# A two-layer diffusion block on one core: the rest of the MoE routing is called for inside the first expert block

## The chip, the cores and the metric

The kernel runs on one core of a Trainium2 chip. The metric is the device time of one execution in microseconds (us); the time of the kernel before is the median of three executions.

## The reference, cut to what matters

Two layers (one with a Mamba-2 mixer over 512 tokens, context and latent, one with a retention mixer over the 256 latent tokens), each of them closed by a hierarchical mixture of experts (MoE) in fp32. The routing of the MoE chooses for every token one group of four, then two of its eight experts:

```
g_sel = jnp.argmax(g_logits, -1)
g_gate = take(jax.nn.softmax(g_logits, -1), g_sel)
e_logits = take(e_logits.reshape(n_tok, 4, 8), g_sel)
top_p, top_i = lax.top_k(jax.nn.softmax(e_logits, -1), 2)
top_w = top_p / jnp.sum(top_p, -1, keepdims=True) * g_gate[:, None]
...
out = (silu(x @ gate[e]) * (x @ up[e])) @ down[e]     # each chosen expert e
ffn = sum over the two choices of top_w * out
```

All 32 experts' weights (6 MB each) are read from HBM in each layer.

## The kernel before, in words

A layer's MoE is an object of class `MoE`: `route()` (line 1535) decides where every token goes, `pairs()` (line 1841) runs over the experts, `finish()` and `norms()` close the layer. Layer 0 has four tiles of 128 tokens (`nt` = 4), layer 1 two.

**Routing.** `route()` starts from the logits `lg` of all tokens. VectorE marks the group and the two experts of each token (lines 1575 to 1597; `goh`, `oh1`, `oh2`, their maxima `gm`, `m1`, `m2`). TensorE counts, by products with a triangle and with ones, the number of each token in its expert's queue (tile `pp`), from which VectorE writes `pos`, the slot of each token at each expert (line 1607). `gather_oh` (line 1688) writes the one-hot matrices `oh` of the first four experts, which always stand at places 0 to 3 (line 1609). `places()` (line 1631) sorts the other experts by load: `to` is the permutation from experts to places, `ppe` the product that gives each place its expert. Then `to_places(pos, True)` (lines 1611 and 1656) brings `pos` into the order of places: four transposes (`pat`), a copy by ScalarE (`aT`), a product with `to` for each tile (`pap`), and one more product whose result is kept as `posT` (`pab`). After it come the softmax weights (lines 1613 to 1624: nine VectorE operations and two exponentials) and `to_places(wt, False)` for the weights (line 1625), and `wr`, the weights split into two parts (line 1627).

**Experts.** `pairs()` goes through blocks of two wide experts (64 slots each) or four narrow ones (32 slots each); `p` is the block's number, two blocks share one set of one-hot matrices `G[g]`. The tokens of a block are gathered by products with the one-hots (`gather`, line 1703, tile `px`, copied to `xT` by ScalarE for the one block and VectorE for the other). For block 0 this is done piecewise ahead of the contraction steps of its own products (line 1886: one eighth ahead of steps k = 0 and 1, two eighths ahead of 2, 4 and 6). `gate_up` (line 1753) has eight steps k, each with the gate and up products (`pg`, `pu`) of the block's experts; then follow `hidden_T`, `down` (`pd`) and, a block later, `add` (`pc`, line 1829). `one_hots(1)` is called for ahead of block 0's `gate_up` (line 1885); its tile has one buffer, which `G[0]` holds until `weights(0)` (`pw`, line 1728) has read it. `blocks()` and `base()` (lines 1919 and 1818) come behind block 0's products; `base` runs on GpSimd.

**Order of the work.** Instructions are put in order by a planner when the kernel is built: each engine takes, in the planner's own reckoning of time, the first instruction in program order that is ready. Operations called through `S.T`, `S.V` and `S.A` (class `InOrder`, line 187; they all show line 194 in the profile) are pinned behind the one that stands ahead of them on their engine; all others may move ahead. All of `route()` is pinned so. PSUM tiles of the tag "mm" (`pp`, `pk`, `ppe`, `pat`, `pap`, `pab`, `px`, `pw`, `pb`, `ph`) share two buffers.

**Weights.** `Ring` (line 124) holds 1 MB slots in several pools; SyncE's queue issues one load (line 173) as soon as the products that read the slot's old content are done. The order of the loads is fixed when the kernel is built, and a load that waits holds up those behind it. Behind block 5 stands a branch on a run-time count (line 2008) that lets overfull experts take more blocks; it is not taken here.

Of the kernel before, what the change touches and what calls it, by code (L numbers as in the profile page):

```python
# [12 lines left out]
F32R = mybir.dt.float32r  # L13
# [3 lines left out]
AF = mybir.ActivationFunctionType  # L17
OP = mybir.AluOpType
AX = mybir.AxisListType
# [3 lines left out]
P = 128  # L23
# [173 lines left out]
def col(S, name, a=0, b=None):  # L197
    o, w = CL[name]
    return S.c[:, o + a:o + (w if b is None else b)]
# [1236 lines left out]
FIRST = ((0, 0), (1,))  # L1436
ROWS_AT = (0,)
ROWS_K = (2, 4)


class Expert:
# [30 lines left out]
class MoE:  # L1472
# [62 lines left out]
    def route(self):  # L1535
# [16 lines left out]
        def red(out, in_, op):  # L1552
            V.tensor_reduce(out, in_, AX.X, op)

        def bc(a, k):
            return a[:, :, None].to_broadcast([P, nt, k])
# [51 lines left out]
        V.tensor_scalar(pos, pos, -1024.0, None, op0=OP.add)  # L1608
        self.G = {0: self.gather_oh([(pos[:, :, 0:FIXED], CAP)], col(S, "i64"), V)}
        self.places(pp[:, nt, :], sb16)  # L1610
        self.pos, self.posT = self.to_places(pos, True)

        d, gsum, p2, rd = new(4), new(), new(4), new(4)
        V.tensor_tensor(d, lg4, bc(gm, 4), OP.subtract)
        AC.activation(d, d, AF.Exp)
        red(gsum, d, OP.add)
        V.tensor_tensor(p2, m2, m1, OP.subtract)
        AC.activation(p2, p2, AF.Exp)
        V.scalar_tensor_tensor(rd, p2, 1.0, bc(gsum, 4), op0=OP.add, op1=OP.mult)
        V.reciprocal(rd, rd)  # L1620
        V.scalar_tensor_tensor(rd, rd, 0.5, goh, op0=OP.mult, op1=OP.mult)
        V.tensor_tensor(oh2, oh2, of_group(p2), OP.mult)
        V.tensor_tensor(oh2, oh2, oh1, OP.add)
        V.tensor_tensor(by_group(wt), oh2, of_group(rd), OP.mult)
        self.wt, _ = self.to_places(wt, False)

        self.wr = sb.tile([P, nt, 2, 32], F32R, name="wr")
        V.tensor_copy(self.wr[:, :, 0], self.wt)
        V.tensor_tensor(self.wr[:, :, 1], self.wt, self.wr[:, :, 0].bitcast(F32), OP.subtract)

    def places(self, cn, sb16):

# [20 lines left out]
        self.expert, self.cn = by[:, 0], by[:, 1]  # L1653
        self.reg = {}

    def to_places(self, a, back):

        S, nt, V, T_ = self.S, self.nt, self.S.V, self.S.T
        pt = self.ps([32, nt, 128], "pat", "mm")
        for i in range(nt):  # L1660
            T_.transpose(pt[:, i], a[:, i], col(S, "ident"))
        aT = self.wk2.tile([32, nt * 128], F32, name="aT", tag="os", bufs=2)
        S.A.activation(aT, pt.rearrange("e t c -> e (t c)"), AF.Copy)
        pa = self.ps([P, nt, 32], "pap", "mm")
        for i in range(nt):
            T_.matmul(pa[:, i], aT[:, i * 128:(i + 1) * 128], self.to[:, :32], start=True, stop=True)
        V.tensor_copy(a, pa)
        if not back:
            return a, None
        pb = self.ps([64, self.T], "pab", "mm")  # L1670
        T_.matmul(pb, self.to, aT, start=True, stop=True)
        t = self.sb.tile([64, self.T], BF, name="posT")
        V.tensor_copy(t, pb)
        V.tensor_tensor(t[32:64], pb[32:64], t[32:64], OP.subtract)
        return a, t
# [165 lines left out]
    def pairs(self):  # L1841
# [20 lines left out]
        def part(g, q, nb=2):  # L1862
            self.gather(G[g], [xT[2 * g], xT[2 * g + 1]], q, nb)
# [5 lines left out]
                weights(g)  # L1869
        start(0)  # L1870
        prev = None

        def after(th, W, os_, w, end=False):
            nonlocal prev
# [6 lines left out]
        for p, places in enumerate(order):  # L1881
            g = p // 2 + 1
            W = [Expert(S, self.layer, e, e == WIDE) for e in places]
            if p % 2 == 0 and g < groups:
                G[g] = one_hots(g)
            th = self.gate_up(W, xT[p], None if p else lambda k: part(0, k, 1) if k < 2 else part(0, k // 2) if k % 2 == 0 else None)
            if p == 0:
                self.spread_rows()
            os_ = self.scatter_oh([S.id2[:, e:e + 1] for e in places], s64 if width(p) == CAP else s32)
            if g < groups:  # L1890
                if p == 0:
                    weights(0)
                    self.blocks()
                    self.base()
                if p % 2 == 0:
                    start(g)
                if p > LATE:
                    ahead(p, g)
            after(th, W, os_, ws[p], p == last)
            if g < groups and p <= LATE:  # L1900
                ahead(p, g)
            if p == EXTRA:
                W = [Expert(S, self.layer, WIDE)]
                pw = self.wk.tile([P, self.nt, 1], F32, name="pw")
                nc.vector.tensor_scalar(pw, self.pos[:, :, WIDE:WIDE + 1], float(-CAP), None, op0=OP.add)
                sw = self.wk.tile([P, 1], F32, name="sw")
                nc.vector.tensor_scalar(sw, s64, float(CAP), None, op0=OP.add)
                x, wx = self.block_tokens(self.gather_oh([(pw, CAP)], i64), self.wt[:, :, WIDE:WIDE + 1])
                c = S.id2[:, WIDE:WIDE + 1]
                osx = self.scatter_oh([c, c], sw)  # L1910
                after(self.gate_up(W, x), W, osx, wx)
            if p == REST:
                self.add(*prev)
                prev = None
                self.rest()
# [288 lines left out]
```

## Time and profile before

| | us |
|---|---|
| median of 3 executions (lowest, highest) | 2083.04 (2081.06, 2083.69) |
| the profiled execution | 2084.03 |
| its span, first to last instruction | 2082.2 |
| TensorE busy | 1827.3 (88%) |
| VectorE, ScalarE, GpSimd busy | 1023.1, 508.4, 516.2 |
| mean granted TensorE clock | 0.944 of full |
| read from HBM | 537.51 MB, 261 GB/s over the span |

The profile is of one execution. Busy shares are means over stages with different limits, so the stage of the change is read by itself: the timeline gives start and length of each group of instructions with the idle time before it and what ended that, the windows give busy time, granted clock and DMA rate of a stretch.

### The profile page before, as it was taken

How to read it: one execution, taken by the hardware profiler on the slowest of the kernel's cores; microseconds unless marked ns; L12 is line 12 of the kernel's file. 1: busy time of each engine (PE TensorE's matmuls, PEld its weight loads, DVE VectorE, ACT ScalarE, POOL GpSimd, SP SyncE). 2: the span in 40 equal slices, each digit the busy share in tenths (PEclk: the TensorE clock that was granted, in tenths of full speed). 3: DMA queues.
4: the chain of work that ended last, by engine and by line, in shares of the span. 5: the costliest groups of instructions: out<-in, count | busy, mean ns of one | idle time of the engine just before them, and what ended most of it. 6: DMA issues, size and time to landing. Idle time of an engine off the chain costs nothing. (4 is left out here: it accounts for less than half of the span.)

```text
span 2082.2 us, 24508 instructions
## 1 busy us (share of the span) xinstructions
PE 1827.3 (88%) x9373; PEld 1057.7 (51%) x9373; DVE 1023.1 (49%) x1790; ACT 508.4 (24%) x885; POOL 516.2 (25%) x332
## 2 busy tenths in 40 slices
PE   7798889889985999989999979898896999878886
PEld 4576667567674433334333368786873433312221
DVE  3868687777586243443333475574444332311112
ACT  2655454544212100000000142332232101100000
POOL 1454645444345000000000053464551100000000
PEclk9899999999995999999999989999997999989998
DMA  7332322234843997799999754464364999999996
GB/s 296 105 122 82 132 102 102 100 133 144 284 162 126 382 402 302 300 393 377 409 409 409 302 176 145 164 238 157 125 238 171 377 412 413 413 367 411 414 413 252
DMA packets 137947, 544.42 MB, mean 261 GB/s; under 512 B 10368, under 2 KB 10880, under 8 KB 125152
## 3 DMA queue, kind: packets, MB, share of 16 engines
q1 hardware_dynamic: 137392, 542.57, 67.5%
q8 instruction: 76, 1.25, 0.2%
q14 instruction: 47, 0.39, 0.0%
q10 hardware_dynamic: 432, 0.21, 0.0%
HBM read 537.51 MB, written 5.24 MB: 261 GB/s over the span
## 5 line engine op out<-in xcount | busy, mean ns | idle before, releaser
L428 POOL TENSOR_TENSOR wl<-ringA,wh 128x1024 fp32r<-128x1024 f32 x117 | 293.5, 2523 | 808.3 <-ACT wh L427 800.2
L427 ACT ACTIVATE wh<-ringA 128x1024 fp32r<-128x1024 f32 x120 | 126.1, 1058 | 189.2 <-issue 46.9
L1765 PE MATMUL pg<-ringB,xT 128*32 128x512 f32 (+1 forms) x348 | 123.2, 600 | 4.1 <-DMA ringB<-in_moe_w_gate_up_dram 3.8
L1774 DVE SCALAR_TENSOR_TENSOR th<-th,pg 128x512 f32<-128x512 f32 (+1 forms) x24 | 16.5, 686 | 224.4 <-ACT th L1770 207.8
L1765 PE MATMUL pu<-ringB,xT 128*32 128x512 f32 (+1 forms) x316 | 119.1, 605 | 4.3 <-SPq L2008 2.8
L1770 ACT ACTIVATE th<-pg 128x512 f32<-128x512 f32 (+1 forms) x24 | 14.3, 596 | 433.5 <-PE pg L1765 422.6
L1837 DVE TENSOR_TENSOR tl<-pc,ringB 128x512 f32<-128x512 f32 x136 | 88.9, 685 | 55.0 <-PE pc L1812 53.4
L1805 DVE SCALAR_TENSOR_TENSOR yh<-pd,ws,yh 128x512 fp32r<-128x512 f32 x40 | 30.0, 751 | 173.5 <-ACT yh L1804 171.6
L2064 POOL TENSOR_TENSOR oacc<-oacc,ringE 128x512 f32<-128x512 f32 x1 | 1.6, 1622 | 451.9 <-ACT oacc L194 451.9
L1794 PE MATMUL pd<-ringE,hT 128*32 128x512 f32 (+1 forms) x360 | 103.7, 618 | 6.0 <-ACT hT L1784 3.4
L1794 PE MATMUL pd<-ringB,hT 128*32 128x512 f32 (+1 forms) x304 | 104.0, 630 | 4.1 <-ACT hT L1784 2.4
L1712 PEld LDWEIGHTS px<-oh,hhl 128*128 128x128 f32 x640 | 81.2, 194 | 37.4 <-issue 36.1
L1171 PE MATMUL pin<-u,wh 128*128 128x256 f32 (+1 forms) x256 | 84.3, 330 | 16.6 <-DVE gT L1223 12.3
L724 DVE SCALAR_TENSOR_TENSOR cacc<-pad,cw,cacc 128x512 f32<-128x512 f32 x96 | 94.1, 983 | 6.8 <-ACT cacc L722 6.1
L1765 PE MATMUL pg<-ringE,xT 128*32 128x512 f32 (+1 forms) x240 | 90.3, 613 | 7.5 <-DMA ringE<-in_moe_w_gate_up_dram 6.2
L1812 PE MATMUL pc<-yh,os 128*128 128x512 f32 (+1 forms) x272 | 89.5, 432 | 6.2 <-DVE tl L1837 5.5
L1765 PE MATMUL pg<-ringA,xT 128*32 128x512 f32 (+1 forms) x220 | 93.1, 615 | 1.9 <-DMA ringA<-in_moe_w_gate_up_dram 1.9
L1765 PE MATMUL pu<-ringE,xT 128*32 128x512 f32 (+1 forms) x240 | 91.6, 606 | 3.0 <-DMA ringE<-in_moe_w_gate_up_dram 3.0
L1765 PE MATMUL pu<-ringA,xT 128*32 128x512 f32 (+1 forms) x204 | 91.1, 610 | 3.0 <-DMA ringA<-in_moe_w_gate_up_dram 3.0
L1712 PE MATMUL px<-oh,hhl 128*128 128x256 f32 (+1 forms) x640 | 91.2, 293 | 0.5 <-DVE wsx L1997 0.5
L1838 DVE TENSOR_TENSOR oacc<-oacc,tl 128x512 f32<-128x512 f32 x136 | 88.5, 684 | 0.7
L1765 PE MATMUL pg<-ringF,xT 128*32 128x512 f32 (+1 forms) x204 | 85.0, 607 | 3.6 <-DMA ringF<-in_moe_w_gate_up_dram 3.3
(407 smaller groups left out, 4432.7 us busy)
## 6 DMA issues: line engine op xcount, KB each, us to landing
ringB<-in_moe_w_gate_up_dram SPq DMA_DIRECT2D x79, 1024.0 KB, 17.1
ringE<-in_moe_w_gate_up_dram SPq DMA_DIRECT2D x60, 1024.0 KB, 17.7
ringA<-in_moe_w_gate_up_dram SPq DMA_DIRECT2D x51, 1024.0 KB, 17.6
ringF<-in_moe_w_gate_up_dram SPq DMA_DIRECT2D x47, 1024.0 KB, 17.8
ringE<-in_moe_w_down_dram SPq DMA_DIRECT2D x43, 1024.0 KB, 17.9
ringA<-in_mod_w_dram SPq DMA_DIRECT2D x40, 1024.0 KB, 4.9
ringB<-in_moe_w_down_dram SPq DMA_DIRECT2D x36, 1024.0 KB, 15.7
ringA<-in_ret_in_w_dram SPq DMA_DIRECT2D x24, 1024.0 KB, 5.0
```

The costliest lines, as they stand in the source:

```text
L427: S.split = nc.scalar.activation(hi, w, AF.Copy).ins
L428: (eng or nc.gpsimd).tensor_tensor(lo, w, hi.bitcast(F32), OP.subtract)
L724: nc.vector.scalar_tensor_tensor(acc, pad[:, :, t:t + 256], cw[:, m, t:t + 1], acc, op0=OP.mult, op1=OP.add)
L1171: self.S.nc.tensor.matmul(p, a, self.uh(k)[:, T], start=k == 0, stop=False)
L1712: nc.tensor.matmul(px[:, b, :], self.S.hhl[i][:, m, j * 128:(j + 1) * 128], oh[:, i], start=i == 0 and m == 0, stop=i == nt - 1 and m == 1)
L1765: nc.tensor.matmul(po[o:o + n, :], xT[:, k, a * n:(a + 1) * n], w.get(k)[:, u * 512:(u + 1) * 512], start=k == 0, stop=k == 7)
L1774: nc.vector.scalar_tensor_tensor(th[:m], th[:m], 1.0, pg[:m], op0=OP.add, op1=OP.mult)
L1794: nc.tensor.matmul(pd[u % n][o:o + m, :], hT[:, j, a * m:(a + 1) * m], w.get(8 + j)[:, u * 512:(u + 1) * 512], start=j == 0, stop=j == 3)
L1805: self.S.nc.vector.scalar_tensor_tensor(yl[:, u], p, ws, yh[:, u].bitcast(F32), op0=OP.mult, op1=OP.subtract)
L1812: self.S.nc.tensor.matmul(pc, os_[s, i * 128:(i + 1) * 128], ys[q][s, u % n], start=q == 0, stop=q == 1)
L1837: V.tensor_tensor(t, pc, self.gate(i)[:, c], OP.mult)
L1838: V.tensor_tensor(self.acc(i)[:, c], self.acc(i)[:, c], t, OP.add)
```

## The change

The two moves to place order and the softmax weights leave `route()` and become a generator, `rest_of_route()`. It is advanced ahead of steps k = 1, 2, 4 and 5 of block 0's gate and up products, behind that step's gather. `to_places` is cut in two (`by_expert` does the transposes and the copy). The operations moved are called through `nc.vector`, `nc.scalar` and `nc.tensor`: they are no longer pinned. `one_hots(1)` is called for behind block 0's products. The number of instructions stays the same.

```diff
+ROUTE_K = (1, 2, 4, 5)
@@ route()
-        self.pos, self.posT = self.to_places(pos, True)
+        self.chosen = lg4, gm, m1, m2, goh, oh1, oh2, new, pos, wt
+
+    def rest_of_route(self):
...
+        V, AC = S.nc.vector, S.nc.scalar
...
+        aT = self.by_expert(pos)
 
         d, gsum, p2, rd = new(4), new(), new(4), new(4)
...
         V.tensor_tensor(by_group(wt), oh2, of_group(rd), OP.mult)
-        self.wt, _ = self.to_places(wt, False)
-
-        self.wr = sb.tile([P, nt, 2, 32], F32R, name="wr")
+        yield
+        self.pos, self.posT = self.to_places(pos, aT, True)
+        yield
+        aT = self.by_expert(wt)
+        yield
+        self.wt, _ = self.to_places(wt, aT, False)
+
+        self.wr = self.sb.tile([P, nt, 2, 32], F32R, name="wr")
         V.tensor_copy(self.wr[:, :, 0], self.wt)
         V.tensor_tensor(self.wr[:, :, 1], self.wt, self.wr[:, :, 0].bitcast(F32), OP.subtract)
+        yield
@@ to_places()
+    def by_expert(self, a):
+
+        S, nt = self.S, self.nt
         pt = self.ps([32, nt, 128], "pat", "mm")
         for i in range(nt):
-            T_.transpose(pt[:, i], a[:, i], col(S, "ident"))
+            S.nc.tensor.transpose(pt[:, i], a[:, i], col(S, "ident"))
         aT = self.wk2.tile([32, nt * 128], F32, name="aT", tag="os", bufs=2)
-        S.A.activation(aT, pt.rearrange("e t c -> e (t c)"), AF.Copy)
+        S.nc.scalar.activation(aT, pt.rearrange("e t c -> e (t c)"), AF.Copy)
+        return aT
+
+    def to_places(self, a, aT, back):
+
+        nt, V, T_ = self.nt, self.S.nc.vector, self.S.nc.tensor
@@ pairs()
+        later = self.rest_of_route()
+
+        def first(k):
+            if k < 2 or k % 2 == 0:
+                part(0, k if k < 2 else k // 2, 1 if k < 2 else 2)
+            if k in ROUTE_K:
+                next(later)
...
-            if p % 2 == 0 and g < groups:
+            if p % 2 == 0 and 0 < p and g < groups:
                 G[g] = one_hots(g)
-            th = self.gate_up(W, xT[p], None if p else lambda k: part(0, k, 1) if k < 2 else part(0, k // 2) if k % 2 == 0 else None)
+            th = self.gate_up(W, xT[p], None if p else first)
             if p == 0:
+                G[1] = one_hots(1)
                 self.spread_rows()
```

## Rows read from the trace of the kernel before

**Rows 1.** Windows: length, PE, PEld, DVE, ACT, POOL busy, PE clock, DMA share, GB/s.

```profile
648.40:668.70 20.30, 11.49 (x42) 8.25 (x42) 11.57 (x50) 3.68 (x6) 6.29 (x3) 0.50 0.54 204
668.70:691.70 23.00, 22.86 (x120) 10.91 (x119) 3.40 (x8) 2.02 (x5) 12.35 (x6) 0.96 0.69 256
...
1579.40:1593.50 14.10, 7.25 (x27) 5.10 (x26) 7.58 (x45) 1.44 (x5) 0.00 (x0) 0.50 0.54 219
```

**Rows 2.** Timeline of layer 0: start, length, engine, line, operation, count, idle before.

```profile
648.83 1.43 DVE L194 TENSOR_TENSOR oh<-c,pos 128x256 fp32r<-128x256 f32 x4
651.49 0.60 PE L194 MATMUL ppe<-pl,c 32*128 32x32 f32 x2 [3.16 <-DVE pl L194]
662.34 1.01 PE L194 MATMUL pat<-c,wt 128*32 128x128 f32 x4 [4.37 <-DVE wt L194]
665.87 2.93 PE L1712 MATMUL px<-oh,hhl 128*128 128x256 f32 x12
668.72 1.12 PE L1765 MATMUL pg<-ringX,xT 128*64 128x512 f32 x1
674.41 2.17 PE L1712 MATMUL px<-oh,hhl 128*128 128x256 f32 x16
692.78 1.71 DVE L1697 TENSOR_TENSOR oh<-c,pos 128x128 fp32r<-128x128 f32 x8 [0.52 <-PE pw L1728]
```

**Rows 3.** Timeline of layer 1.

```profile
1579.80 0.76 DVE L194 TENSOR_TENSOR oh<-c,pos 128x256 fp32r<-128x256 f32 x2
1591.50 2.08 PE L1712 MATMUL px<-oh,hhl 128*128 128x256 f32 x8
1593.51 1.98 PE L1765 MATMUL pg<-ringF,xT 128*64 128x512 f32 x4
1615.33 1.08 PE L1765 MATMUL pg<-ringE,xT 128*64 128x512 f32 x4 [0.47 <-ACT xT L1718]
```

**Rows 4.** PE groups by shape, 647 to 669 us, then 1578 to 1592 us: busy, mean, idle.

```profile
L194 PE MATMUL pap<-pl,aT 32*128 32x32 f32 x16 | 3.8, 399 | 1.4 <-ACT aT L194 1.4
L194 PE MATMUL pab<-aT,pl 32*64 32x512 f32 x2 | 2.0, 1083 | 0.0
...
L194 PE MATMUL pap<-pl,aT 32*128 32x32 f32 x8 | 2.1, 402 | 0.9 <-ACT aT L194 0.9
L194 PE MATMUL pab<-aT,pl 32*64 32x256 f32 x2 | 1.1, 656 | 0.0
L194 PE MATMUL pat<-c,wt 128*32 128x128 f32 x2 | 0.6, 396 | 3.5 <-DVE wt L194 3.5
```

**Rows 5.** SyncE's queue: the first weight load that each MoE's products set free.

```profile
674.50 0.37 SPq L173 DMA_DIRECT2D ringX<-in_moe_w_gate_up_dram  x1
...
1598.11 7.35 SPq L173 DMA_DIRECT2D ringF<-in_moe_w_gate_up_dram  x3
```

**Rows 6.** Windows of the expert blocks of both layers, columns as in rows 1.

```profile
690.00:820.00 130.00, 124.59 (x641) 54.27 (x637) 53.04 (x118) 11.97 (x22) 0.00 (x0) 0.98 0.98 389
820.00:840.00 20.00, 20.00 (x99) 10.68 (x99) 2.94 (x4) 1.98 (x3) 0.00 (x0) 0.93 0.32 106
840.00:860.00 20.00, 20.00 (x80) 6.05 (x76) 9.51 (x16) 1.57 (x3) 0.00 (x0) 0.97 0.60 233
...
1640.00:1850.00 210.00, 187.22 (x965) 70.71 (x962) 62.86 (x126) 19.42 (x35) 0.00 (x0) 0.98 1.03 413
```

**Rows 7.** PE's waits from 690 to 820 us, the longest: total, times, longest.

```profile
PE ph L1782 <- DVE th L1775: 2.9, 2, 1.6
```

**Rows 8.** Timeline of GpSimd and VectorE, layer 1, then GpSimd's `base` of layer 0.

```profile
1572.58 0.30 DVE L194 TENSOR_TENSOR xT<-xT 128x64 f32<-128x64 f32 x2
1573.12 4.69 POOL L194 TENSOR_TENSOR hhl<-tok,hhl 128x1024 fp32r<-128x1024 f32 x2 [1.17 <-ACT hhl L194]
1573.36 2.19 DVE L194 TENSOR_TENSOR xT<-xT 128x64 f32<-128x64 f32 x1
...
662.41 4.66 POOL L1825 TENSOR_TENSOR oacc<-oacc,ringB 128x1024 f32<-128x1024 f32 x2 [18.35 <-ACT ringB L1822]
```

More of the change, by code (lines that the diff above doesn't have):

```diff
@@ L1610, in route @@
         self.places(pp[:, nt, :], sb16)
-        self.pos, self.posT = self.to_places(pos, True)
+        self.chosen = lg4, gm, m1, m2, goh, oh1, oh2, new, pos, wt
+    def rest_of_route(self):
+        S, nt = self.S, self.nt
+        V, AC = S.nc.vector, S.nc.scalar
+        lg4, gm, m1, m2, goh, oh1, oh2, new, pos, wt = self.chosen
+        by_group = lambda a: a.rearrange("p t (g e) -> p t g e", g=4)
+        of_group = lambda a: a[..., None].to_broadcast([P, nt, 4, 8])
+        aT = self.by_expert(pos)
         d, gsum, p2, rd = new(4), new(), new(4), new(4)
-        V.tensor_tensor(d, lg4, bc(gm, 4), OP.subtract)
+        V.tensor_tensor(d, lg4, gm[:, :, None].to_broadcast([P, nt, 4]), OP.subtract)
         AC.activation(d, d, AF.Exp)
-        red(gsum, d, OP.add)
+        V.tensor_reduce(gsum, d, AX.X, OP.add)
         V.tensor_tensor(p2, m2, m1, OP.subtract)
         AC.activation(p2, p2, AF.Exp)
-        V.scalar_tensor_tensor(rd, p2, 1.0, bc(gsum, 4), op0=OP.add, op1=OP.mult)
+        V.scalar_tensor_tensor(rd, p2, 1.0, gsum[:, :, None].to_broadcast([P, nt, 4]), op0=OP.add, op1=OP.mult)
         V.reciprocal(rd, rd)
@@ L1654, in places @@
         self.reg = {}
-    def to_places(self, a, back):
-        S, nt, V, T_ = self.S, self.nt, self.S.V, self.S.T
+    def by_expert(self, a):
+        S, nt = self.S, self.nt
         pt = self.ps([32, nt, 128], "pat", "mm")
         for i in range(nt):
-            T_.transpose(pt[:, i], a[:, i], col(S, "ident"))
+            S.nc.tensor.transpose(pt[:, i], a[:, i], col(S, "ident"))
         aT = self.wk2.tile([32, nt * 128], F32, name="aT", tag="os", bufs=2)
-        S.A.activation(aT, pt.rearrange("e t c -> e (t c)"), AF.Copy)
+        S.nc.scalar.activation(aT, pt.rearrange("e t c -> e (t c)"), AF.Copy)
+        return aT
+    def to_places(self, a, aT, back):
+        nt, V, T_ = self.nt, self.S.nc.vector, self.S.nc.tensor
         pa = self.ps([P, nt, 32], "pap", "mm")
```

## The prediction

> **What bounds the kernel now.** I read the windows around the start of each MoE first, then the timeline inside them, then the groups of TensorE there, SyncE's queue, and the windows of the blocks behind. The 20.3 us between the counting products and block 0's first gate product in layer 0 show TensorE busy for 11.49 us at a clock of 0.50 (its lower level, 1.2 GHz); the 23 us behind them show it busy for 22.86 us at 0.96 (nearly all at 2.4 GHz). Layer 1 has the same gap: 14.1 us, 7.25 busy, clock 0.50 [rows 1]. The gap is a chain on one strand: the timeline of layer 0 has TensorE waiting 3.16 us for VectorE's sorting (`ppe`), then 4.37 us for the softmax weights (`pat`), and only then the gathers, which have had their one-hots since 650.26 us (648.83 + 1.43) but start at 665.87; the first product is at 668.72 [rows 2]. In layer 1 the one-hots are there at 1580.56, the gathers start at 1591.50, the first product at 1593.51 [rows 3]. The two waits for `aT`, 1.4 us in all in layer 0 and 0.9 in layer 1, belong to the same chain [rows 4].
>
> All weight slots are full by then: the next load goes out only when block 0's step 1 is done, at 674.50 and at 1598.11 [rows 5]. So the gap holds up TensorE and the weight stream alike. Behind it layer 0 is TensorE's up to the branch (124.59 of 130 us busy beside 389 GB/s; then the stream falls to 106 and 233 GB/s for 40 us in which TensorE is never idle), while layer 1 is the stream's from 1640 us (413 GB/s, TensorE idle for 23 of 210 us) [rows 6]. The waits of TensorE before layer 0's branch name no DMA; their longest total is 2.9 us, for VectorE's `th` [rows 7]. An earlier block 0 is therefore kept to the branch in layer 0, and moves the whole stream in layer 1.
>
> **The change, step by step.**
>
> *Gathers ahead of the moves, layer 0.* The first eight gather products need the one-hots, 650.26 us, and a free "mm" buffer, which the counting tiles give back at about the same time. Eight take 8/12 of 2.93 = 1.95 us [rows 2]. `ppe` takes some 1.0 us of TensorE beside them, its input is ready a little before 651.49 [rows 2]. Both are done by 650.3 + 1.95 + 1.0 = 653.3, the copy of the gather lies beside `ppe`. The first product starts at 653.3 in place of 668.72: **15.4 us** earlier. Bounds: half a microsecond to either side, as the planner puts `ppe` behind or ahead of the gathers.
>
> *The same, layer 1.* Four gather products make one eighth of the block here: half of 2.08 = 1.04 us from 1580.56 [rows 3]; then `ppe`, whose input comes as in layer 0 (651.49 - 650.26) some 1.2 us after the one-hots. First product near 1582.8 in place of 1593.51: **10.7 us** earlier.
>
> *What now stands inside the block.* TensorE is full there [rows 1], so every product moved in costs its length. At the low clock the two `pat` are 1.01 each, the two `pap` together 3.8, `pab` 2.0 [rows 2, 4]: 7.8 us in layer 0. In layer 1 two `pat` at 0.6, `pap` 2.1, `pab` 1.1 make 4.4 [rows 4]. Most of them will run at the higher clock. How much shorter they are there no row shows; the nearest is the gather, 2.93/12 = 0.244 us at the low level and 2.17/16 = 0.136 at the high [rows 2], a factor 0.56. That gives 7.8 x 0.56 = **4.4 us** and 4.4 x 0.56 = **2.5 us**; bounds 3.9 to 7.8 and 2.2 to 4.4 (half, and unchanged). In layer 1 both eighths of the gather ran ahead of the first product, now one runs inside: 1.04 x 0.56 = **0.6 us** (0.5 to 1.0).
>
> *Products at the low clock.* The block's mean clock of 0.96 in layer 0 [rows 1] is (1 - 0.96)/0.5 x 23 = 1.8 us at the low level, which cost half of that, 0.9 us. Ahead of the rise TensorE had not paused since the weights' `pap` (`pat` ends at 663.35 [rows 2], a wait of 0.7 follows), some 6.5 us. If it rises after as much work again, counted from 650.3, all of step 0 now runs low. Four records take 1.98 us low, 1.08 high [rows 3], and a step has eight: 1.8 us lost in place of 0.9. **0.9 us** per layer (0 to 1.8).
>
> *VectorE and ScalarE.* The nine VectorE operations and two exponentials of the softmax are no longer pinned and depend only on the selection, so the planner may put them into the sorting chain that `ppe` waits for. Not shown before. Bound: 0 if they fill pauses, and 2 us if each lengthens the chain by some 0.2; I take **0.5 us** per layer, near the lower end, since dependent operations leave VectorE such pauses. Otherwise they hide under the 11 us that TensorE needs to step 4, where `wt` is first read; without that cover TensorE's queue stops there and with it the products of steps 4 to 7.
>
> *Waits in the new places.* TensorE works its queue in order, so if a `pat` or `pap` stands ahead of its input (`aT`, a freed "mm" buffer), the block's products stand behind it, and behind them the first freed weight slot. The nearest row is 1.4 us for two waits [rows 4], 0.7 each; five tiles are put in per layer. Bound 0 to 3.5 us per layer; I take 0, because the planner fills such pauses with other products: of the block's 23 us today, with a copy behind each gather, 0.14 are idle [rows 1].
>
> *`one_hots(1)` behind the block.* Its eight operations ran at 692.78, released by `pw` [rows 2]: the single buffer, not the call, set their time. Nothing. Without that cover they would be late by their own 1.7 us, still ahead of block 2's gathers. *Queues.* No DMA is moved; SyncE's loads keep their order and follow TensorE. GpSimd's `base` keeps its place.
>
> *Sum.* Layer 0: 15.4 - 4.4 - 0.9 - 0.5 = 9.6. Layer 1: 10.7 - 2.5 - 0.6 - 0.9 - 0.5 = 6.2. Together 15.8 us off the profiled execution's 2084.0, 2068.2; the median of the runs is 1.0 lower, so **2067 us**. With every cost at its dear end, the waits too: layer 0 15.4 - 0.5 - 7.8 - 1.8 - 2 - 3.5 = -0.2, layer 1 10.7 - 0.5 - 4.4 - 1.0 - 1.8 - 2 - 3.5 = -2.5, that is no gain at all (2086); with every one at its cheap end 15.4 + 0.5 - 3.9 = 12.0 and 10.7 + 0.5 - 2.2 - 0.5 = 8.5, 2062.5.
>
> **The rivals.**
>
> *The moved chain meets `base` on VectorE (half the gain).* In layer 1 a VectorE operation with two SBUF operands took 2.19 us beside GpSimd's `hhl`, where two like it took 0.30 together just before [rows 8]. Layer 0's `base` is eight GpSimd operations from 662.41, the first two 4.66 us [rows 8]: 18.6 us in all. Seven softmax operations have two such operands: 7 x 2.3 = 16 us if the planner leaves them beside `base`, and the copies that free the gathers' buffers queue behind them. Then block 0 of layer 0 waits until its gain is gone: 2083 - 6.2 = 2077. Against it: they are ready before 650 us, `base` must first wait for its row and ScalarE. By the Trainium skill, "SBUF — State Buffer", "Who interferes with whom", a VectorE instruction with two SBUF inputs and a GpSimd one that reads SBUF hold each other up whole; the row agrees. By that rule alone the time would be this rival's.
>
> *The order stays what it was (no change).* The moved transposes are ready before the one-hots; if they get the two free "mm" buffers first, the gathers stand behind them as now, and only the softmax wait goes into the block. Then 4.4 + 3.5 of waits could go, but the move of `pos` still leads: between 2075 and 2083, I take 2081. Against it: the planner takes the first ready instruction in program order, and the gathers now come first.
>
> *The weight stream loses more at the branch (slower).* Loads are queued in a fixed order, and one that waits holds the rest. The lull at layer 0's branch costs (413 - 106)/413 x 20 + (413 - 233)/413 x 20 = 23.6 us of the full rate that layer 1 shows [rows 6]. A new order of the products from block 1 on is laid out with the new times; if it opens one more lull like it where TensorE then waits, 23.6 - 15.8 = 7.8 us are lost: 2091. It decides from 16 us of added lull; below that there is still a gain. For it: every instruction behind the change may be placed anew. Against it: nothing in blocks 1 to 5 depends on the change, and today's lull costs TensorE no idle time.
>
> **How the numbers follow.** The forecast has 0.76, `base` 0.07, the old order 0.08, the lull 0.09. A measurement tells about 0.2% of this kernel from no change, 4.2 us. Faster: the forecast less 0.03 for its dear ends, and the `base` case, 0.80; same: the old order and 0.02 of the dear ends, 0.10; slower: the lull and 0.01 of the dear ends, 0.10. The range leaves out the lull, the old order and the dear ends, 0.20 together: 2059 (the cheap end, with 3 us for a kinder new order) to 2079 (two thirds of the sum lost, the `base` case within).
>
> **What would show it.** Right: in the timeline, gathers at about 650.5 and 1580.6, first gate products near 653 and 1583, the first load of each MoE near 660 and 1589 (14 and 9 us earlier); `pat`, `pap`, `pab` between the gate products at about half their length; block 0's last product 9 to 10 us earlier in layer 0, 6 in layer 1; the same DMA rates behind. Wrong: a TensorE wait for `aT`, `wt` or a copy inside block 0; softmax operations of over 2 us; first loads earlier but the branch of layer 0, or the stream's end, at the old time.

## The result, and the profile after

The changed kernel took 2071.18 us in the median (2067.77 to 2072.24, five runs) beside 2081.6 for the kernel before (2078.29 to 2083.69): a ratio of 0.9945, 95% interval 0.9931 to 0.996. It is faster by 0.55%, and the forecast of 2067 us was 4 us too low. The profiled execution took 2067.77 us, with a span of 2066.0.

The timeline of TensorE in layer 0, which answers to [rows 2] (start, length, line, operation):

```profile
648.01 0.18 PE L194 MATMUL pp<-sb,lt_bf 128*128 128x32 bf16 x1 [11.26 <-DVE sb L194]
651.97 0.60 PE L194 MATMUL ppe<-pl,c 32*128 32x32 f32 x2 [3.23 <-DVE pl L194]
652.92 2.93 PE L1733 MATMUL px<-oh,hhl 128*128 128x256 f32 x12
655.78 1.11 PE L1786 MATMUL pg<-ringX,xT 128*64 128x512 f32 x1
656.69 0.63 PE L1786 MATMUL pg<-ringX,xT 128*64 128x512 f32 x1
658.69 0.60 PE L1677 MATMUL pat<-c,pos 128*32 128x128 f32 x4
663.18 1.07 PE L1687 MATMUL pap<-pl,aT 32*128 32x32 f32 x8
664.18 1.07 PE L1786 MATMUL pg<-ringE,xT 128*64 128x512 f32 x2
665.18 1.07 PE L1692 MATMUL pab<-aT,pl 32*64 32x512 f32 x2
668.38 1.44 PE L1786 MATMUL pu<-ringE,xT 128*64 128x512 f32 x3
669.76 2.17 PE L1733 MATMUL px<-oh,hhl 128*128 128x256 f32 x16
683.38 0.83 PE L1749 MATMUL pw<-wr,oh 128*128 128x4 f32 x6
```

The gathers now follow `ppe` at once, and the moved products stand between the gate and up products. From the counting products (`pp`) the first gate product is 7.8 us away; it was 21.1 (668.72 - 647.60) [rows 2]. In layer 1 it is 5.8 us away, where it was 14.5 (1593.51 - 1578.98) [rows 3]. The lines for this are `pp` of both layers and `ph` of layer 0 before, then `ph` of layer 0 and the start of layer 1 after; `ph` are the transposes in `hidden_T`, which close block 0:

```profile
647.60 0.18 PE L194 MATMUL pp<-sb,lt_bf 128*128 128x32 bf16 x1 [11.07 <-DVE sb L194]
695.47 0.63 PE L1782 MATMUL ph<-c,th 128*128 128x128 f32 x4
1578.98 0.19 PE L194 MATMUL pp<-sb,lt_bf 128*128 128x32 bf16 x1 [8.18 <-DVE sb L194]
...
687.34 0.66 PE L1803 MATMUL ph<-c,th 128*128 128x128 f32 x4
1567.71 0.19 PE L194 MATMUL pp<-sb,lt_bf 128*128 128x32 bf16 x1 [9.04 <-DVE sb L194]
1573.51 1.76 PE L1786 MATMUL pg<-ringF,xT 128*64 128x512 f32 x4
```

Two things differ from what was forecast: the gathers are behind `ppe`, not in the 3.2 us pause ahead of it, and `pab` has come between the two experts' products of step 2. SyncE's queue shows the freed slots, as [rows 5] did:

```profile
661.18 0.37 SPq L173 DMA_DIRECT2D ringX<-in_moe_w_gate_up_dram  x1
...
1578.78 10.31 SPq L173 DMA_DIRECT2D ringF<-in_moe_w_gate_up_dram  x3
```

Against `pp` these loads come 13.7 and 8.1 us earlier than before; 14 and 9 were forecast.

The same sections by window (columns as in [rows 1]): layer 0 up to the first gate product, its block up to `pw`, then the two for layer 1, then the later stretches of [rows 6] with a clock time some 10 us earlier:

```profile
648.01:655.78 7.77, 4.54 (x34) 4.16 (x33) 5.17 (x24) 0.28 (x1) 0.00 (x0) 0.50 1.01 375
655.78:683.38 27.60, 27.42 (x145) 13.68 (x144) 12.41 (x28) 5.00 (x8) 18.62 (x8) 0.98 0.71 276
...
1567.71:1573.51 5.80, 3.18 (x18) 2.80 (x17) 3.38 (x22) 0.28 (x1) 0.00 (x0) 0.50 1.02 420
1573.51:1606.78 33.27, 32.39 (x121) 11.83 (x120) 11.30 (x29) 8.09 (x14) 9.31 (x4) 0.93 0.58 214
...
810.00:830.00 20.00, 20.00 (x102) 11.01 (x103) 2.85 (x4) 1.98 (x3) 0.00 (x0) 0.94 0.36 118
830.00:850.00 20.00, 20.00 (x80) 5.87 (x80) 9.96 (x16) 1.63 (x4) 0.00 (x0) 0.98 0.65 245
1629.00:1839.00 210.00, 188.17 (x957) 70.01 (x952) 62.54 (x126) 19.44 (x35) 0.00 (x0) 0.95 1.02 413
```

The block stays full (27.42 of 27.60 us), the lull at the branch has the rates of before (118 and 245 GB/s), and the last stretch is bound by the same stream of 413 GB/s. The longest wait of TensorE in layer 0's later blocks is the one of [rows 7] again, 2.9 us in all for `th`. The groups of the moved products, layer 0 and then layer 1, for [rows 4] (the `pat` of the slots takes as long as that of the weights):

```profile
L1687 PE MATMUL pap<-pl,aT 32*128 32x32 f32 x16 | 2.1, 274 | 0.0
L1692 PE MATMUL pab<-aT,pl 32*64 32x512 f32 x2 | 1.1, 612 | 0.0
...
L1687 PE MATMUL pap<-pl,aT 32*128 32x32 f32 x8 | 1.3, 276 | 0.0
L1692 PE MATMUL pab<-aT,pl 32*64 32x256 f32 x2 | 0.6, 400 | 0.0
L1677 PE MATMUL pat<-c,wt 128*32 128x128 f32 x2 | 0.4, 270 | 0.0
```

And VectorE's timeline: the last operation of the softmax weights, the one-hots, and the first operation of the split of the weights (`wr`) deep in the block:

```profile
648.52 0.29 DVE L1634 TENSOR_TENSOR wt<-xT 128x128 f32<-128x128 f32 x1
649.30 1.43 DVE L194 TENSOR_TENSOR oh<-c,pos 128x256 fp32r<-128x256 f32 x4
...
675.71 2.45 DVE L1643 CAST wr<-wt 128x128 fp32r<-128x128 f32 x1
```

**Reading executions stage by stage.** In the profiles of the changed kernel and its variants `pp` of layer 0 comes anywhere from 642.5 to 650.5 us, the same kernel at 648.0, 650.1 and 644.8 in three executions. Most of that scatter lies ahead of the route, and so of the change. Distances such as +7.8 are us behind `pp` of the same layer. The table at the end of the experiments gives two stages that leave it out: from `pp` of layer 0 to `pp` of layer 1, and from there to the end of the span. Before they are 1578.98 - 647.60 = 931.4 and 2082.2 - 1578.98 = 503.2 us; after, 919.7 and 498.3. Each is read from one execution.

### The profile page after: what moved, and what is told of

Same layout as the page of the kernel before. It is cut to its first block, busy times and chain, and to the rows that moved or that the text cites. A ratio compares the mean times of both kernels' runs of the same rounds, so it can differ in the third digit from the quotient of the medians.

```text
span 2066.0 us, 24508 instructions
## 1 busy us (share of the span) xinstructions
PE 1823.8 (88%) x9373; PEld 1055.2 (51%) x9373; DVE 1031.5 (50%) x1790; ACT 508.6 (25%) x885; POOL 515.9 (25%) x332
## 5 line engine op out<-in xcount | busy, mean ns | idle before, releaser
L1791 ACT ACTIVATE th<-pg 128x512 f32<-128x512 f32 (+1 forms) x24 | 14.3, 597 | 434.5 <-PE pg L1786 412.7
L2093 POOL TENSOR_TENSOR oacc<-oacc,ringE 128x512 f32<-128x512 f32 x1 | 1.6, 1620 | 451.6 <-ACT oacc L194 451.6
L1171 PE MATMUL pin<-u,wh 128*128 128x256 f32 (+1 forms) x256 | 83.8, 328 | 12.9 <-DVE gT L1223 10.0
```

The costliest lines, as they stand in the source:

```text
L1171: self.S.nc.tensor.matmul(p, a, self.uh(k)[:, T], start=k == 0, stop=False)
```

## The experiments

Every variant is an edit of the changed kernel, and a ratio is to the kernel before, timed on the same chip.

**again**: no edit.

> The changed kernel once more, unaltered. The two profiled executions differ by 16.2 us, the medians by 10.4 us. If the change is worth what the starts of the two expert stages show (block 0 ends 8.5 us earlier in layer 0, and layer 1 gains some 5 us from its counting products to its end), the medians should come out 11 to 15 us below the kernel before. If the smaller figure of the first medians is the truth and the rest of the profiled difference is drift of the clock, 9 to 11 us. In the profile: first gate product 7.8 us behind the counting products in layer 0 and 5.8 us in layer 1, as in the first profile, and in layer 1 a stretch of the lower clock inside block 0 again if that belongs to the change.

2069.71 us, ratio 0.9938 (0.9922 to 0.9955). The gain stands, a little larger than in the first timing.

**ahead**: the whole moved chain is called for ahead of block 0, but still without pins.

```diff
-        later = self.rest_of_route()
+        for _ in self.rest_of_route():
+            pass
...
-            if k in ROUTE_K:
-                next(later)
```

> All moved steps are called for ahead of block 0 instead of inside it; they stay unpinned, and one_hots(1) stays behind the block. Theory (the place in the order of TensorE counts): transposes and products of both moves stand ahead of the gathers again; only the wait for the softmax weights goes, since they are ready early on VectorE. First gate product some 15 to 16 us behind the counting products in layer 0 (21.1 before, 7.8 after) and 10 to 11 in layer 1 (14.5 before, 5.8 after); time 4 to 6 us above the changed kernel, 2075 to 2077. Rival (losing the pins is what counts, the planner then puts the gathers first by itself): first gate products as in the changed kernel and the same time within 2 us.

2074.69 us, 0.9966 (0.9948 to 0.9983). Without its pins the softmax costs nothing on the path (no wait of 4.37 us as in [rows 2]), but the moves still do. The timeline of `ahead`, layer 0:

```profile
653.30 1.03 PE L1677 MATMUL pat<-c,pos 128*32 128x128 f32 x4
655.01 1.91 PE L1687 MATMUL pap<-pl,aT 32*128 32x32 f32 x8 [0.68 <-ACT aT L1679]
...
662.30 2.93 PE L1733 MATMUL px<-oh,hhl 128*128 128x256 f32 x12
```

Each moved product takes its full length at the low clock here (`pap` 1.91, 1.07 inside the block), with two waits of 0.68 us for `aT` between them (the second, like the second `pap`, is left out here): 9.0 us from `pat` to the gathers. So of the gain of 13.4 us (2083.08 - 2069.71) 8.4 come without the moves' new place, near the two waits for `wt` of 4.37 and 3.5 us [rows 2, 4], and 5.0 from that place. The intervals of the two ratios overlap a little; the stages in the table below, 5.0 to 5.5 us longer in sum than in `again` and `again_two`, say the same.

**layer0_only**: in layer 1 the chain is pinned in the route, as before.

```diff
+        if self.layer == 1:
+            self.pinned_rest()
...
-            if k in ROUTE_K:
+            if k in ROUTE_K and self.layer == 0:
```

> Layer 1 is routed as before (pinned, ahead of block 0), layer 0 as in the changed kernel. Theory (both layers keep their gains, in layer 1 by the weight stream): 4 to 6 us above the changed kernel, so 6 to 9 us below the kernel before. Rival (layer 1 ends by its weight stream, so its start is worth nothing): the same as the changed kernel.

2074.1 us, 0.9964 (0.9952 to 0.9977), 4.4 us over `again`. Layer 1's landmarks are those of before to 0.01 us, and its stage takes 503.3 us, as before. Both layers keep what they win.

**weights_inside** and **weights_again** (the same kernel twice): the move of the slots pinned in the route, that of the weights inside block 0.

```diff
+        self.pos, self.posT = self.to_places(pos, self.by_expert(pos, True), True, True)
...
-        self.pos, self.posT = self.to_places(pos, aT, True)
```

> Only the softmax weights and their move are called for inside block 0; the move of the slots stays pinned in the route, ahead of the gathers, as in the kernel before. Theory (what pays is that the chain stands behind the first gathers, both moves alike): the first gate product stands some 13 us behind the counting products in layer 0 and 9 us in layer 1 (7.8 and 5.8 in the changed kernel, 16.8 and 11.2 with the whole chain ahead), about half of the 5.0 us that the whole chain ahead cost is lost: 2072 us. Rival (the wait for the softmax was all that paid, the move of the slots is as dear inside the block as ahead of it): as the changed kernel, 2069.7 us.

> weights_inside once more, unchanged: its profiled execution (2073.2 us) was the fastest of six with a median of 2077.0, so its profile did not show where the rest went. Theory (part of the executions lose another 2 to 4 us to the clock in layer 1's first block, as in the run ahead): 2074 to 2077 us, and a profiled execution nearer to that shows the stretch with a clock of 0.8 or less. Rival (a slower start of the program, ahead of the route): the layers last 923.4 and 498.6 us as in the first profile, and the counting products of layer 0 come later than 650 us.

2077.04 us, 0.9969 (0.9957 to 0.9981), then 2075.44, 0.9955 (0.9938 to 0.9971): theory and rival of the first text were both too kind. The first gate product comes at +12.9 in layer 0, between the two as expected, but `pw` at +38.4 and +38.6, close to `ahead` (+39.0) and not to `again` (+36.0). Half of the chain inside wins little (in layer 1 1 to 2 us against `ahead`). In layer 0 the first gate product comes 3.9 us earlier than in `ahead`, but 1.7 us go to the products that now stand inside (`pat` 0.60, `pap` 1.07), and 1.6 to 1.9 us to the clock, which over the first 8 us of the block was 0.79 and 0.75, in `ahead` 0.99. That leaves 0.3 to 0.6 us, as measured at `pw`. The timeline of `weights_inside` also shows the gathers of two more eighths placed between step 0 and step 1 in one piece, which puts off the first freed slot:

```profile
664.87 0.95 PE L1786 MATMUL pu<-ringX,xT 128*64 128x512 f32 x1
665.76 3.14 PE L1733 MATMUL px<-oh,hhl 128*128 128x256 f32 x24
```

The second profile settled the question of `weights_again` only in part: its stages are 925.0 and 499.7 us, 2.7 us longer than in the first, and the clock in layer 1's block was at 1.00 after its rise, so neither the fall of the clock there nor the late start that the rival wanted (`pp` at 649.2) is borne out. In layer 1 the rise itself came later: the clock over the first 8 us of the block was 0.71, in the first profile 0.86, that is 1.2 us lost, beside the 1.0 by which the stage is longer. The 1.6 us of layer 0 stay open.

**odd_steps**: the moved parts behind other steps.

```diff
-ROUTE_K = (1, 2, 4, 5)
+ROUTE_K = (1, 3, 5, 6)
```

> The same work inside block 0, but the moved parts stand behind steps 1, 3, 5 and 6 in place of 1, 2, 4 and 5, so that in layer 0 no moved product comes between the products of the two experts of one step. Theory (two experts' products run side by side, and a product put between them makes the first of them run alone, about 1 us each time): in layer 0 the block's product pw 1 us earlier against the counting products than in the changed kernel (34.4 in place of 35.4 to 36.0), layer 1 unchanged, since there the rows of the slots still stand between pairs: 2068.7 us. Rival (the place inside the block is without effect): pw at 35.4 to 36.0, 2069.7 us.

2068.29 us, 0.9933 (0.9914 to 0.9952). The whole time can't tell that from `again`. `pw` of layer 0 comes at +34.0, expected +34.4, but that landmark has moved by itself: its eight products now stand in two groups of four, with two gate products between them. The next landmark, `ph`, comes at +38.8, in the six profiles with the changed kernel's layer 0 at +38.9 to +40.4. What the order is worth shows in a stretch that holds the same products in both kernels, from the first `pap` to the gathers ahead of step 4:

```profile
660.73 1.07 PE L1687 MATMUL pap<-pl,aT 32*128 32x32 f32 x8
...
666.47 2.18 PE L1733 MATMUL px<-oh,hhl 128*128 128x256 f32 x16
```

It takes 5.7 us here and 6.6 in after (663.18 to 669.76): 0.8 us. The pair that was split in the changed kernel now stays together, and `pap` and `pab` stand between whole steps. The fence with the timeline of after shows the split: two `pg` of `ringE` took 1.07 alone at 664.18, `pab` followed, and three `pu` were left over at 668.38; side by side the products of two experts take 0.59 each and end together.

**gather_first**: the first eighth's gathers are called ahead of `ppe`, in a PSUM buffer of the tag "pd" in place of "mm".

```diff
+        self.x0 = [self.wk.tile([P, 8, P], F32, name="xT", bufs=3) for _ in range(2)]
+        self.gather(self.G[0], self.x0, 0, 1, "pd")
...
-        start(0)
+        xT[0], xT[1] = self.x0
```

> As the changed kernel, but the gather of the first eighth is called for ahead of the product ppe and has a PSUM buffer of its own, so that it runs while TensorE waits 3.2 us for the sorting. Theory (the prediction's first product came 2.4 us late because the planner put ppe and its wait ahead of the gathers): first gate product 5.0 to 5.8 us behind the counting products in layer 0 (7.8 in the changed kernel) and 4 to 5 in layer 1 (5.8), and 2 to 4 us off the time. Rival (the block is then held by the copies or by the lower clock, which it meets with more of its products): first products earlier, but block 0 ends at the same distance from the counting products, 35.4 and 36.0 us, and the time is the same within 1 us.

2074.66 us, 0.9968 (0.9957 to 0.9979): 5 us slower than `again`, although the gathers now stand ahead of `ppe`, as the prediction had reckoned. The timeline of `gather_first`, layer 1:

```profile
1572.88 1.97 PE L1788 MATMUL pg<-ringF,xT 128*64 128x512 f32 x2 [0.43 <-ACT xT L1741]
1574.78 0.63 PE L194 MATMUL ppe<-pl,c 32*128 32x32 f32 x2
1576.68 2.76 PE L1788 MATMUL pu<-ringF,xT 128*64 128x512 f32 x3
```

`ppe` came between the products of step 0; these then ran one after the other at the low clock, 6.5 us from 1572.88 to the end of the last `pu` at 1579.44. Behind that the clock fell once more (0.62 from 1585 to 1594 us, TensorE busy throughout), and `ph` came at +46.5, in `again` at +40.8. So the loss is layer 1's; in layer 0 `ph` came earlier than in any other profile, at +37.4. Which of the two, the order of step 0 or the clock, cost how much, the next two runs were to tell.

**gather_apart**: as `gather_first`, with step 0 pinned behind `ppe`, and the moved parts and the rows of the slots at other steps. **gather_pairs**: the same, with the rows where the changed kernel has them.

```diff
-ROWS_K = (2, 4)
-ROUTE_K = (1, 2, 4, 5)
+ROWS_K = (5, 7)
+ROUTE_K = (1, 3, 5, 6)
...
+                    T_ = self.S.T if before and k == 0 else nc.tensor
```

> The gathers of the first eighth ahead of the sums of the sorting, as in the run gather_first, which lost 5.0 us against the changed kernel although its first product came 3 us earlier; now the products of step 0 are kept together (pinned behind the sums), the moved parts stand behind steps 1, 3, 5 and 6, the rows of the slots behind 5 and 7. Theory (gather_first lost by products put between the pairs and by the low clock that followed; without them its earlier start is kept): first gate product 5 to 6 us behind the counting products in layer 0 and 4 to 5 in layer 1, pw 33.5 or less in layer 0, 2067 us. Rival (the start with the gathers first makes the engine stay at its lower clock longer, whatever the order of the pairs): as gather_first, 2073 to 2075 us.

> As gather_apart, but with the rows of the slots behind steps 2 and 4 as in the changed kernel, so that base stands where it stood. Theory (gather_apart lost in layer 1 only by the 5.35 us for which ph waited for VectorE beside base, and the low clock behind it; the earlier start was kept up to there, pw at +35.9 in place of +38.4 to +39.1): no wait at ph, ph some 38.5 to 39.5 us behind the counting products of layer 1, the layer 496 us to the end, layer 0 920.5 us between the two counting products: 2067 us. Rival (the start with the gathers first costs by itself): as gather_apart, 2075 us.

`gather_apart`: 2075.38 us, 0.996 (0.9948 to 0.9973), no better than `gather_first`. `gather_pairs`: 2070.31 us, 0.9931 (0.9917 to 0.9945). So the gathers first don't cost by themselves, and the late rows cost what `gather_apart` lost (below). In layer 1 `ph` came at +40.6, 5.9 us ahead of `gather_first`; (1 - clock) x length from the first gate product to +41 makes 2.9 us lost here and 8.3 there (0.92 and 0.78), so nearly all of it is the clock. Why that was lower in `gather_first` is not shown. Nor do they win here: in layer 0 the first gate product is at +4.9, 2.9 us ahead of the changed kernel, yet `ph` at +38.6 is only 0.2 ahead of `odd_steps`. Its timeline says why:

```profile
655.07 1.11 PE L194 MATMUL pg<-ringX,xT 128*64 128x512 f32 x1
...
658.68 1.66 PE L1735 MATMUL px<-oh,hhl 128*128 128x256 f32 x8
660.71 0.64 PE L1789 MATMUL pg<-ringX,xT 128*64 128x512 f32 x1
```

All of step 0 runs at the low clock (1.11 and less a product, 0.59 to 0.64 behind it), and the full one comes during the gathers at 658.68, 8.5 to 10.2 us behind `pp`. In the profile of after it came with the second pair of step 0, at 656.69, 8.7 us behind `pp`. So here the higher clock came no earlier with the earlier start, and what was put ahead of it ran at half speed: over the first 8 us of the block the clock was 0.71, in `odd_steps` 0.96, 2.0 us of the 2.9. That is not so each time. With the changed kernel's layer 0 the clock rose between +7.8 or sooner (`layer0_only`, `base_on_vector`) and +10.9 (`again_two`, `rows_late`), and in `gather_first`, which also starts early, at about +5.4; its layer 0 has the earliest `ph`. What the early start is worth thus depends on when the clock rises, and what decides that no run here shows.

**rows_late**: only the rows of the slots, small products of layer 1, behind steps 5 and 7. **base_on_vector**: the same, with `base` of layer 1 on VectorE.

```diff
-ROWS_K = (2, 4)
+ROWS_K = (5, 7)
...
-        S, G = self.S, self.S.nc.gpsimd
+        S, G = self.S, self.S.nc.gpsimd if self.nt == 4 else self.S.nc.vector
```

> As the changed kernel, but the rows of the slots, small products of layer 1 that already stood inside block 0, come behind steps 5 and 7 in place of 2 and 4, away from the moved products. Theory (rows and moved products close together let TensorE's granted clock fall inside layer 1's block 0 in some executions, 2 to 4 us each time, and split pairs of products): layer 1 from its counting products to the end 496 us in place of 498, and no stretch of block 0 in layer 1 under 0.9 behind the first rise: 2067.5 us. Rival (the fall has another cause, the place of the rows is without effect): 498 us, 2069.7 us, with a fall as often as not.

> As rows_late, but in layer 1 the four operations of base run on VectorE in place of GpSimd (layer 0 as before). In rows_late the four one-hots (oh) of VectorE that had taken 0.90 us took 6.78 us while GpSimd's base stood beside them from 1599.70 to 1609.06, the product ph waited 5.34 us for the reduction behind them, and the granted clock was 0.75 to 0.82 afterwards. Theory (the two engines shut each other out, and base had come into the one place where VectorE is on TensorE's path): with base off GpSimd the one-hots take 0.9 us, ph waits 1 us at most, layer 1 from its counting products to the end 497 to 499 us in place of 505, 2067 us. Rival (the late rows themselves hold the product, whoever does base): ph waits some 5 us again, 2073 us.

`rows_late`: 2073.18 us, 0.9958 (0.9945 to 0.9971), slower than `again` where it was to be faster. Its timeline, layer 1:

```profile
1609.80 1.09 PE L1803 MATMUL ph<-c,th 128*128 128x128 f32 x4 [5.34 <-DVE ws L1755]
...
1602.63 6.78 DVE L1718 TENSOR_TENSOR oh<-c,pos 128x128 fp32r<-128x128 f32 x4 [0.46 <-PE pw L1749]
...
1599.70 4.67 POOL L1846 TENSOR_TENSOR oacc<-oacc,ringB 128x1024 f32<-128x1024 f32 x2 [38.32 <-ACT ringB L1843]
1604.32 4.74 POOL L1847 TENSOR_TENSOR oacc<-oacc,ringB 128x1024 f32<-128x1024 f32 x2
```

`base` follows the rows, so in layer 1 it moved with them, into the stretch in which VectorE makes the next one-hots. Four of these, from two SBUF operands each, end only when GpSimd is done; TensorE waits 5.34 us behind them, and its clock is lower when it goes on (0.75 from 1612 to 1620 us; in `again` 1.00). The one-hots in `base_on_vector`:

```profile
1605.59 0.90 DVE L1718 TENSOR_TENSOR oh<-c,pos 128x128 fp32r<-128x128 f32 x4 [0.78 <-PE pw L1749]
...
1607.12 1.23 DVE L1847 TENSOR_TENSOR oacc<-oacc,ringB 128x1024 f32<-128x1024 f32 x1
```

0.90 us, no wait at `ph`, layer 1 at 498.6 us in place of 505.2, and 2067.89 us in all, 0.9928 (0.9914 to 0.9941). The theory holds and its rival falls. An operation of `base` also takes 1.23 us on VectorE where GpSimd needs 2.33 (4.67 for two).

**again_two**: the changed kernel once more beside these.

> The changed kernel once more, beside the two versions that may beat it, on the same chip. Theory and rival alike: ratio to the kernel before 0.9935 to 0.995, 2068 to 2072 us.

2070.53 us, 0.9937 (0.9924 to 0.995). No variant beats it by more than the intervals allow; `base_on_vector` (0.9928), `gather_pairs` (0.9931) and `odd_steps` (0.9933) may by up to 2 us. The stages of all profiles, in us (L0 from `pp` of layer 0 to `pp` of layer 1, L1 from there to the end):

| | L0 | L1 | sum | ratio |
|---|---|---|---|---|
| before | 931.4 | 503.2 | 1434.6 | 1 |
| after | 919.7 | 498.3 | 1418.0 | 0.9945 |
| again | 922.2 | 497.7 | 1419.8 | 0.9938 |
| again_two | 923.0 | 497.3 | 1420.3 | 0.9937 |
| ahead | 924.8 | 500.6 | 1425.3 | 0.9966 |
| layer0_only | 923.2 | 503.3 | 1426.5 | 0.9964 |
| weights_inside | 923.4 | 498.6 | 1422.0 | 0.9969 |
| weights_again | 925.0 | 499.7 | 1424.7 | 0.9955 |
| odd_steps | 920.4 | 499.9 | 1420.3 | 0.9933 |
| gather_first | 920.8 | 503.0 | 1423.8 | 0.9968 |
| gather_apart | 920.7 | 502.4 | 1423.1 | 0.996 |
| gather_pairs | 920.5 | 498.4 | 1418.9 | 0.9931 |
| rows_late | 921.8 | 505.2 | 1427.1 | 0.9958 |
| base_on_vector | 921.8 | 498.6 | 1420.4 | 0.9928 |

The same kernel differs by up to 3.3 us in a stage (after and again_two, L0), so a difference of 1 or 2 us between two rows says nothing by itself. About half of this difference is the clock behind block 0, near the branch. The stretch from 110 to 200 us behind `pp` of layer 0, before and after (columns as in [rows 1]):

```profile
757.60:847.60 90.00, 84.60 (x392) 36.19 (x394) 30.15 (x62) 7.33 (x13) 0.00 (x0) 0.94 0.80 312
...
758.01:848.01 90.00, 84.93 (x412) 35.77 (x407) 30.78 (x64) 8.08 (x14) 0.00 (x0) 0.98 0.79 304
```

The clock dips there for a few us at a time, three times in before, once in after and twice in `again` and `again_two` (0.96 each). (1 - clock) x 90 makes 5.4 us lost in before, 1.8 in after and 3.6 in the other two.

## Why the prediction was right, and where it was off

**What bounds the kernel** held. Both layers won, each by itself (`layer0_only`), and what block 0 won arrived at the end: L0 9.2 us shorter in `again`, 8.4 in `again_two`, 11.7 in after (forecast 9.6), L1 5.6, 5.9 and 4.9 (forecast 6.2). The sum is 14.3 to 16.6 us, forecast 15.8. In the medians it is 10.4 in the first timing and 13.4 and 13.3 in the later ones. So the stages come out nearer to the forecast than the time does, and part of that is luck: the one profile of before had more dips of the clock near the branch than these three of after, worth 3.6, 1.8 and 1.8 us. Without them the sum is 12.5 to 13.0 us in all three. How many dips the other executions of before had is not known.

**The step that failed: gathers ahead of `ppe`.** 15.4 and 10.7 us were forecast, against `pp` it was 21.1 - 7.8 = 13.3 and 14.5 - 5.8 = 8.7: 2.1 and 2.0 us too much. The planner put the gathers behind `ppe`, and the pause of 3.2 us ahead of it is still there. In layer 0 the one-hots were ready at +2.7 (649.30 + 1.43) and `ppe` started at +4.0, so 1.2 us of the pause were lost; and twelve gather products stand ahead of the first gate product where eight had been reckoned with, 0.9 us more (2.86 - 1.95). In layer 1 it is seven in place of four, 1.8 us that no longer lie in the pause. The bound of half a microsecond for the planner's choice was too narrow: it reckoned with the 1.0 us of `ppe` alone. `gather_pairs`, which mends this, hardly gains: over the first 8 us of its block 0 the clock was 0.71, in before 0.90, which is 1.5 us more lost than before. The forecast had this as 0.9.

**Moved products**: 4.4 us in layer 0, as forecast (2.1 + 1.1 + 0.6 + 0.6), 2.7 in layer 1 (forecast 2.5). The factor from the gathers was right. The second eighth of layer 1's gather, for which 0.6 us was forecast inside the block, ran ahead of it but for one product of eight.

**Products at the low clock**: 0.9 us per layer was forecast as an added loss. Over the first 8 us of layer 0's block the clock was 0.90 before, 0.94 in after, 0.86 in `again`, 0.81 in `again_two` and 1.00 in `layer0_only` and `base_on_vector`, whose layer 0 is the changed kernel's. That is 0.8 us lost before, and 0.5, 1.1, 1.5 and 0 with the change. So the term lies between a gain of 0.8 and a loss of 0.7, different from one execution to the next.

**VectorE and ScalarE**: 0.5 us each was forecast. The softmax went into the chain of selection and sorting, ended ahead of the slots (648.52 + 0.29), and `ppe` came at +3.96 in place of +3.89, in layer 1 at +3.06 in place of +2.81. Behind `pp` it cost 0.1 and 0.3 us. Ahead of `pp`, where these distances don't reach, TensorE waited 11.07 us before and 11.26 after in layer 0, 0.2 us more. In layer 1 that wait was 8.18 before, in seven of the later profiles 8.2 to 8.3 and in six 9.0 to 9.1. In these six an addition of VectorE (`tok`) took 3.25 us beside one of GpSimd, in the others 1.2; it stands ahead of any softmax operation. **Waits**: none in block 0 of layer 0, 0.7 us for `xT` in layer 1 (0.47 before [rows 3]), as forecast but for that.

**Not foreseen**: the pair of products split by `pab`, 0.8 us in layer 0 (`odd_steps`). With it the account of layer 0 closes, in us gained against before:

| | after | again | again_two |
|---|---|---|---|
| first gate product against `pp` | 13.3 | 13.3 | 13.3 |
| moved products inside | -4.4 | -4.4 | -4.4 |
| split pair | -0.8 | -0.8 | -0.8 |
| low clock, first 8 us of the block | +0.3 | -0.3 | -0.7 |
| sum | 8.4 | 7.8 | 7.4 |
| measured at `ph`, the block's end | 8.5 | 7.9 | 7.5 |
| measured, whole stage L0 | 11.7 | 9.2 | 8.4 |

So block 0 gave 7.5 to 8.5 us in these three (9.0 in `layer0_only` and `base_on_vector`, which lost nothing to the low clock) where 9.6 were forecast. That the stage came out near 9.6 all the same is owed in the main to the dips near the branch (3.6, 1.8 and 1.8 us more in before); the sum of both is within 0.9 us of each stage. In layer 1 `ph` came 4.0 to 4.7 us earlier and the stage was 4.9 to 5.9 shorter; where that last us comes from was not traced.

**The rivals.** The moved chain beside `base`: the hold-up is real here (the two operations of `wr` took 2.45 and 2.36 us beside it; a `wr` cast of 128x64 with nothing beside it took 0.20 in `gather_apart`, one beside `base` 2.36 in after), but in the changed kernel the softmax is done long before `base` starts at 661.79, and `wr` has until `pw`. `rows_late` shows what the rival would have cost had it met the path: 5.3 us of waiting in one layer, more with the clock behind it. By the Trainium skill, "SBUF — State Buffer", "Who interferes with whom", a VectorE instruction with two SBUF inputs and a GpSimd one that reads SBUF exclude each other; the one-hots of 6.78 and 0.90 us agree. (The cast of `wr` has one SBUF input, so this sentence does not cover it; the trace shows that it was held up.) In layer 1 the moved chain did meet GpSimd: in six profiles, `again` among them, one softmax operation of 128x8 took 2.3 us beside `hhl`, one of the prediction's signs of being wrong. It cost next to nothing there: in `again` the wait for `pp` was 8.22 us, before 8.18, when another VectorE operation stood in that place for 2.31. The old order didn't stay. The weight stream lost nothing at the branch: 118 and 245 GB/s there [rows 6].

## What to carry to other kernels

Work taken off a serial chain and put into a full stretch of TensorE costs its length there. It paid here for two reasons: the waits of the chain went (8.4 us in `ahead`), and the products ran at the higher clock inside (4.4 us in layer 0 in place of 7.8). An earlier start is worth its full length only where the clock rises with it; in `weights_inside` and `gather_pairs` the low clock took some 2 of the 4 and 3 us won at the start. Two products that the profile shows running at the same time should stay neighbours in TensorE's order; here `pab`, put between the products of two experts, made them run one after the other and cost 0.8 us. And whatever is tied to a moved instruction moves with it: look for the place to which a GpSimd operation goes, and whether VectorE is on the path there.

## What the runs showed of the hardware

**The granted clock fell in a stretch without a pause.** Windows of after, layer 1, columns as above:

```profile
1580.00:1584.00 4.00, 4.00 (x14) 1.21 (x14) 1.46 (x5) 0.91 (x2) 0.00 (x0) 1.00 0.94 356
1584.00:1588.00 4.00, 4.00 (x12) 1.25 (x11) 0.00 (x0) 0.60 (x1) 0.00 (x0) 0.65 0.39 157
```

TensorE was busy for all 8 us up to 1588, and yet the clock went from 1.00 to 0.65, partly at its lower level. The fall came right behind the rows of the slots, products over 16 partitions:

```profile
1581.96 1.12 PE L194 MATMUL row<-tl,c 16*128 16x512 f32 x2
```

It was so in seven of the thirteen profiles of the changed kernel and its variants, each time within 4 us behind the first or second group of these rows (`rows_late` and `base_on_vector`, whose rows stand elsewhere, among them), while `again` and `again_two` have the same order without a fall. It costs (1 - 0.65) x 4 = 1.4 us in the second of these windows, 0.38 x 9 = 3.4 in `gather_first`. That the rows are its cause was not tried (by leaving them out, for one). They are not the whole of it: one of the dips near the branch of layer 0, where no such rows run, also fell into a stretch without a pause, here in the kernel before:

```profile
837.00:841.00 4.00, 4.00 (x13) 1.30 (x14) 1.44 (x2) 0.60 (x1) 0.00 (x0) 0.58 0.08 33
```

The cause stays open.
